# Attention scores of 64 rows per head, rebuilt as split products on all 128 rows

## The chip, the cores and the metric

The kernel runs on one core of a Trainium2 chip. A core has a matrix engine (TensorE, PE in the profile, with its weight loads listed apart as PEld), a vector engine (DVE), a scalar engine (ACT), GpSimd (POOL) and a queue that issues transfers (SP). Each engine works through its own instructions in order and waits on semaphores for the others. The metric is device time in microseconds (us), the median of the runs shown; lower is better.

## The reference

Two transformer blocks are computed for 256 tokens of width 2048, in float32. Only the two places where attention scores are formed matter here.

```python
# first block: 32 heads of 64, 4 key heads, window of 128, a sink per head
scores = jnp.einsum('bnqhgd,bnkhd->bnhgqk', q, kb) * (HEAD_DIM ** -0.5)
...
# second block, latent attention: 16 heads, a plain part of 128 and a rope part of 64
sc = (jnp.einsum('bqhd,bkhd->bhqk', qn, k_nope).astype(jnp.float32)
      + jnp.einsum('bqhr,bkr->bhqk', qr, k_rope).astype(jnp.float32)) * scale
```

In the first block the sum under a score runs over 64 numbers. In the second it runs over 128 and then over 64 more, whose key part (`k_rope`) is the same for all heads. A second attention in the second block (heads of 128) is not touched.

## The kernel before

**Layout.** Activations are kept transposed: a tile has 128 features on its rows (partitions) and the 256 tokens along it. A unit is a tile of 128 x 512, which holds two such halves, or the high part of one half beside its low part; there is a pool of 67 units (`NU`). In the first block one half of `q_a` holds two heads below each other, the first on rows 0 to 63 and the second on rows 64 to 127. In the second block one half of `q_r` holds the rope parts of two heads in the same way.

**Products.** The large products do not run in plain float32. Each operand is split into a high part, rounded to a shorter float type (F32R), and a low part, the rest; the product is the sum of high x high, high x low and low x high. A float32 product, where one is still used, is carried out by the compiler as two rows of the trace, a split one as one row. Weights come from memory in chunks (`w_raw`), ACT casts the high part (`w_hi`, L84) and DVE subtracts it to get the low part (`w_lo`, L85); each has four buffers of eight 128 x 128 tiles. `mm` (L195) issues every matmul, so most PE rows carry that one line; the names tell them apart. In a row such as `ps_g<-h,w_hi` the result lies in one of four PSUM banks of the kind g; scores go to two banks of the kind s, and transposes and the products with v to two banks of the kind t.

**Order of the work.** The gemms form one long stream on PE. Attention is put between their matmuls by `Interleave`: an attention is a Python generator, and after every so many weight tiles (`between.every`) one of the waiting generators is taken a step further. A scheduler under the kernel then places each engine's instructions in an order of its own, except for the few that are pinned; this order is fixed when the kernel is built.

**The steps that are touched.** `first_norm` (L455) scales keys into `k_a`, which holds four key heads, and values into `v_a`. `attend_a` (L470) is called 16 times, each for two heads: four score matmuls on 64 rows, two per head (queries 0 to 127 against keys 0 to 127, queries 128 to 255 against all 256), then `exps` (L396: DVE adds the bias and finds the smallest value, ACT takes the exponential), transposes and products with v. The two heads of a call stand on different rows and are issued in turn, the one behind the other. `attend_m` (L688) is called 8 times for two heads: first the plain part on 128 rows (`k_n`, `q_n`), then the rope part on 64 rows (`kr`, which lies in the tile `rb2_kr`, and `q_r`), added in the same bank. `norms` (L665) rotates `kr`, `rope_q` (L720) rotates `q_r`. `split_scaled` (L228) is the helper that writes a high part with ACT and a low part with DVE.

Of the kernel before, what the change touches and what calls it, by code (L numbers as in the profile page):

```python
# [9 lines left out]
F32 = mybir.dt.float32  # L10
# [157 lines left out]
def block_kernel(ctx, tc, order, w, xt, cols, bc, fg, cst, out):  # L168
# [227 lines left out]
    def exps(ps, table, scale, negmax, sums, init):  # L396
# [9 lines left out]
        return t  # L406

    def transposed(p, on_act=False):

        ps = bank("t")  # L410
        for j in range(3):
            nc.tensor.transpose(out=ps[:, j * P:j * P + P], in_=p[:, j * P:j * P + P], identity=ident)  # L412
        pt = unit("prob_t")[:, 0:384]
        if on_act:
            nc.scalar.copy(out=pt, in_=ps[:, 0:384])
        else:
            nc.vector.tensor_copy(out=pt, in_=ps[:, 0:384])
        return pt
# [32 lines left out]
    negsink = const.tile([P, 32], F32, name="negsink")  # L451
    k_a = unit("k_a")
    v_a = unit("v_a")

    def first_norm():  # L455
        for i in range(8):
            sq.add(x_t[i])
            if i % 2:
                yield
        nc.vector.tensor_copy(out=r_a, in_=rstd(sq.sums(), D))  # L460
        yield 2
        rows(r_a, rb)
        yield
        for j in range(2):
            scaled(half(k_a, j), ps_k[j], rb)
        for tb in range(2):
            nc.scalar.activation(out=half(v_a, tb), in_=half(ps_v, tb), func=AF.Copy, scale=r_a[:, tb:tb + 1])
        pin(nc.vector.tensor_scalar(out=negsink, in0=sinks, scalar1=-1.0, scalar2=None, op0=ALU.mult))

    def attend_a(j, q, o):  # L470
# [5 lines left out]
        pp = [bank("s") for _ in range(2)]  # L476
        for a, b, n in ((0, P, P), (P, S, S)):
            for e, ps in enumerate(pp):
                rng = slice(64 * e, 64 * e + 64)
                mm(ps[:, a:a + n], q[rng, a:b], k_a[rng, kt * S:kt * S + n], a == 0, a > 0)  # L480
        for e, ps in enumerate(pp):
# [32 lines left out]
    for j in range(16):  # L514
# [7 lines left out]
        for i, b in ((0, ps_0), (1, ps)) if j == 1 else ((j, ps),):  # L522
            if i % 2 == 0:
                q, o = unit("q_a"), unit("o_a")
                o_a.append(o)
            scaled(half(q, i), b, rb)
            between.add(attend_a(i, half(q, i), half(o, i)))

# [85 lines left out]
    rb2_kr = unit("rb2_kr")  # L614
    rb_2, kr = rb2_kr[:, 0:S], rb2_kr[:, S:]
    rb_lat = unit("rb_lat")
    rb_kv, rb_q = rb_lat[:, 0:S], rb_lat[:, S:]
# [47 lines left out]
    def norms(ps):  # L665
# [11 lines left out]
        yield  # L677
        rotate(kr)
    between.add(norms(ps))
    between.apart = 1  # L680
# [6 lines left out]

    def attend_m(j, qn, qr, kn, v):  # L688

        while j // 2 not in roped:  # L690
            yield
        negmax, sums, rec = sm("negmax"), sm("sums"), sm("rec")
        pp = [bank("s") for _ in range(2)]
        for e, ps in enumerate(pp):
            mm(ps[:, 0:P], qn[e][:, 0:P], kn[e][:, 0:P], True, False)
            mm(ps[:, P:384], qn[e][:, P:S], kn[e], False, False)
        for a, b, n in ((0, P, P), (P, S, S)):
            for e, ps in enumerate(pp):
                rng = slice(64 * e, 64 * e + 64)
                mm(ps[:, a:a + n], qr[rng, a:b], kr[rng, 0:n], False, a > 0)  # L700
        p = [exps(ps, tab_m, scale_m, negmax[:, 2 * e:2 * e + 2], sums[:, 2 * e:2 * e + 2], BIG)
# [18 lines left out]
    def rope_q(u, qr):  # L720
        yield
        for i in range(2):
            rotate(half(qr, i))
        roped.add(u)

    roped = set()

    for u in range(4):
# [20 lines left out]
        for i in range(4):  # L749
# [4 lines left out]
            if i % 2:  # L754
                between.add(attend_m(2 * u + i // 2, [half(qn[-1], e) for e in range(2)], half(qr, i // 2),
                                     [half(kn[i // 2], e) for e in range(2)],
# [314 lines left out]
```

## Time and profile before

| what | value |
|---|---|
| median of the runs shown | 2041.04 us (3 runs, 2039.53 to 2041.19) |
| the profiled execution's own time | 2042.15 us |
| its span, first to last instruction | 2040.4 us |
| granted TensorE clock, mean | 0.996 |
| PE busy | 2014.4 us, 99% of the span |
| DVE busy | 1304.3 us, 64% |
| ACT busy | 1071.6 us, 53% |
| transfers from memory | 360.98 MB, 178 GB/s over the span |

A group of rows in the profile names the line, the engine, the operation, result and operands, the shape of each and their count, and behind the bar the busy time, the mean time of one in ns, and the idle time of the engine ahead of them. In a timeline each row is a run of equal instructions: when the first starts, how long until the last ends, and how many there are. Matmul rows overlap, since the next starts before the last has ended; what one costs is therefore read from start to start, not from its own duration.

### The profile page before, as it was taken

What the parts mean: (1) busy time and instruction counts of PE and PEld (TensorE: products, weight loads), DVE (VectorE), ACT (ScalarE), POOL (GpSimd) and SP (SyncE); (2) the same over time, 40 slices, a digit from 0 to 9 for tenths busy, and PEclk for the clock granted to TensorE, in tenths of its full rate; (3) what the DMA queues carried; (4) which work ended last, traced back from release to release, by engine and by line L of the source; (5) the groups of instructions that cost most, each with busy time, mean ns of one, the idle gap of its engine ahead of it and who ended that gap; (6) DMA issues with size and microseconds to landing.
All of it is one profiled execution on the core that took longest, in us unless ns stands there. A gap on an engine that the chain in (4) does not pass through costs nothing.

```text
span 2040.4 us, 28289 instructions
## 1 busy us (share of the span) xinstructions
PE 2014.4 (99%) x11290; PEld 1744.5 (85%) x11290; DVE 1304.3 (64%) x2129; ACT 1071.6 (53%) x1818; POOL 19.2 (1%) x25
## 2 busy tenths in 40 slices
PE   7999999999999999999999999999999999999998
PEld 6787888888888888888888888888888888888886
DVE  6768865887766655566575767666666666555543
ACT  6767655656545444455465445464445554444443
POOL 0000000000000000000000000000000000000000
PEclk9999999999999999999999999999999999999999
DMA  7343456353444555545545555545555555555553
GB/s 295 119 152 128 166 186 232 109 186 125 149 159 171 186 186 187 193 171 174 183 166 186 187 193 193 185 173 187 189 193 194 187 186 187 191 220 186 196 196 103
DMA packets 53667, 364.89 MB, mean 179 GB/s; under 512 B 6240, under 2 KB 7136, under 8 KB 10400
## 3 DMA queue, kind: packets, MB, share of 16 engines
q1 hardware_dynamic: 52560, 361.07, 49.5%
q8 instruction: 88, 1.44, 0.3%
q0 software_dynamic: 400, 1.31, 0.2%
q10 hardware_dynamic: 576, 0.72, 0.1%
q14 instruction: 43, 0.35, 0.1%
HBM read 360.98 MB, written 2.10 MB: 178 GB/s over the span
## 4 chain that ended last, share of the span: by engine, by line
PE 96%; DVE 1%; ACT 1%; issue 1%; DMA 0%; SPq 0%; POOL 0%; POOLq 0%; ACTq 0%; DVEq 0%
PE ps_g L195 89%; PE ps_s L195 5%; PE ps_t L195 2%; PE ps_t L412 1%; DMA w_raw<-w 0%; ACT prob L404 0%; DVE w_lo L85 0%; ACT w_hi L84 0%; PE ps_t L810 0%; PE ps_t L906 0%; POOL rstd L277 0%; PE ps_t L786 0%; DVE prob L400 0%; DVE prob L496 0%; SPq L217 0%
## 5 line engine op out<-in xcount | busy, mean ns | idle before, releaser
L85 DVE TENSOR_TENSOR w_lo<-w_raw,w_hi 128x1024 fp32r<-128x1024 f32 (+1 forms) x676 | 825.6, 1222 | 320.0 <-ACT w_hi L84 289.9
L84 ACT CAST w_hi<-w_raw 128x1024 fp32r<-128x1024 f32 (+1 forms) x676 | 708.3, 1048 | 352.7 <-PE ps_g L195 269.6
L195 PE MATMUL ps_g<-h,w_hi 128*128 128x512 f32 x3064 | 750.1, 393 | 8.1 <-ACT w_hi L84 6.7
L195 PEld LDWEIGHTS ps_g<-h,w_hi 128*128 128x128 f32 x3064 | 561.9, 189 | 120.2 <-ACT w_hi L84 6.7
L195 PEld LDWEIGHTS ps_g<-h,w_lo 128*128 128x128 f32 x3064 | 395.2, 191 | 20.3 <-issue 4.0
L195 PE MATMUL ps_g<-h,w_lo 128*128 128x256 f32 x3064 | 408.4, 284 | 0.9 <-DVE k_a L198 0.9
L195 PE MATMUL ps_g<-w_hi,act 128*128 128x512 f32 x704 | 216.8, 389 | 0.0
L195 PEld LDWEIGHTS ps_g<-w_hi,act 128*128 128x128 f32 x704 | 132.1, 188 | 27.5
L381 ACT COPY ffn<-ps_g 128x256 f32<-128x256 f32 x86 | 31.8, 373 | 200.9 <-PE ps_g L195 200.9
L195 PE MATMUL ps_g<-w_lo,act 128*128 128x512 f32 x352 | 136.9, 389 | 0.0
L198 DVE TENSOR_TENSOR ffn<-ffn,ps_g 128x256 f32<-128x256 f32 x86 | 36.0, 421 | 144.4 <-ACT ffn L381 144.4
L195 PE MATMUL ps_g<-w_hi,h 128*128 128x512 f32 x256 | 79.4, 389 | 0.0
L195 PEld LDWEIGHTS ps_g<-w_lo,act 128*128 128x128 f32 x352 | 66.1, 188 | 13.7
L404 ACT ACTIVATE prob<-prob,negmax 128x128 f32<-128x128 f32 (+1 forms) x128 | 56.7, 445 | 24.1 <-DVE negmax L400 23.5
L195 PE MATMUL ps_g<-y_m,w_hi 128*128 128x512 f32 x256 | 63.8, 391 | 0.0
L195 PE MATMUL ps_g<-y_d,w_hi 128*128 128x512 f32 x256 | 61.2, 391 | 0.0
L195 PE MATMUL ps_g<-g,w_hi 128*128 128x512 f32 (+1 forms) x240 | 57.8, 377 | 0.0
L195 PEld LDWEIGHTS ps_g<-w_hi,h 128*128 128x128 f32 x256 | 48.1, 188 | 9.9
L195 PE MATMUL ps_g<-mg,w_hi 128*128 128x512 f32 x224 | 56.0, 391 | 0.0
L195 PEld LDWEIGHTS ps_g<-y_d,w_hi 128*128 128x128 f32 x256 | 47.0, 188 | 9.1
L195 PEld LDWEIGHTS ps_g<-y_m,w_hi 128*128 128x128 f32 x256 | 47.0, 188 | 9.1
L195 PE MATMUL ps_g<-c,w_hi 128*128 128x512 f32 x208 | 53.6, 400 | 0.0
(238 smaller groups left out, 1859.2 us busy)
## 6 DMA issues: line engine op xcount, KB each, us to landing
w_raw<-w SPq DMA_DIRECT2D x337, 1024.0 KB, 4.8
w_raw<-w SPq DMA_DIRECT2D x5, 512.0 KB, 7.8
out<-x2n SPq DMA_DIRECT2D x8, 256.0 KB, 3.1
x_t<-xt SPq DMA_DIRECT2D x7, 256.0 KB, 7.8
fgt<-fg POOLq DMA_DIRECT2D x4, 256.0 KB, 5.5
w_raw<-w SPq DMA_DIRECT2D x2, 256.0 KB, 4.6
x_t<-xt SPq DMA_DIRECT2D x2, 128.0 KB, 3.2
lam<-bc POOLq DMA_DIRECT2D x1, 256.0 KB, 6.1
```

The lines of the kernel that those rows point to most:

```text
L84: a = nc.scalar.copy(out=hi[:, q], in_=src[:, q])
L85: b = nc.vector.tensor_tensor(out=lo[:, q], in0=src[:, q], in1=hi.bitcast(F32)[:, q], op=ALU.subtract)
L195: nc.tensor.matmul(out=o, lhsT=a, rhs=b, start=start, stop=stop, skip_group_check=True)
L198: nc.vector.tensor_tensor(out=o, in0=a, in1=b, op=op)
L381: nc.scalar.copy(out=o, in_=ps[:, S:])
L404: nc.scalar.activation(out=t[:, a:b], in_=t[:, a:b], func=AF.Exp, scale=-1.0, bias=negmax[:, qb:qb + 1], accum_out=sums[:, qb:qb + 1])
L412: nc.tensor.transpose(out=ps[:, j * P:j * P + P], in_=p[:, j * P:j * P + P], identity=ident)
```

## The change

For each half of a query tile, the new helper `stacked` writes a unit `q_s` with one half per head. The head's 64 rows are cast to the high part in place (ACT), and the low part is written by DVE on the other 64 rows. So high and low parts of one head stand below each other on 128 rows. Keys get the matching form once: each key head has a unit (`k_s0` to `k_s3`) whose first half is the high part on both sets of 64 rows, and whose second half is the low part on both sets. For the rope part `kr`, which already stands twice below itself, a plain `split_scaled` gives `kr_s`. `stacked_scores` multiplies the stacked queries with the high keys and then with the low keys. This covers all four products of high and low parts.

Per call of an attention, 4 float32 matmuls on 64 rows become 8 split ones on 128 rows: 4 with 128 columns of keys and 4 with 256. In the trace that is 8 rows against 8.

```diff
--- before.py
+++ after.py
@@ -405,6 +405,23 @@
                                  accum_out=sums[:, qb:qb + 1])
         return t
 
+    def stacked(src):
+
+        t = unit("q_s", F32R)
+        for e in range(2):
+            own, other = slice(64 * e, 64 * e + 64), slice(64 - 64 * e, 128 - 64 * e)
+            hi = t[own, e * S:e * S + S]
+            nc.scalar.copy(out=hi, in_=src[own])
+            nc.vector.tensor_tensor(out=t[other, e * S:e * S + S], in0=src[own], in1=hi.bitcast(F32),
+                                    op=ALU.subtract)
+        return [t[:, 0:S], t[:, S:]]
+
+    def stacked_scores(ps, q, k, first):
+
+        for a, b, n in ((0, P, P), (P, S, S)):
+            for o in (0, S):
+                mm(ps[:, a:a + n], q[:, a:b], k[:, o:o + n], first and a + o == 0, a + o > S)
+
     def transposed(p, on_act=False):
 
         ps = bank("t")
@@ -449,7 +466,7 @@
     r_a = const.tile([P, 2], F32, name="r_a")
     rb = unit("rb_a")[:, 0:S]
     negsink = const.tile([P, 32], F32, name="negsink")
-    k_a = unit("k_a")
+    kk = []
     v_a = unit("v_a")
 
     def first_norm():
@@ -461,8 +478,15 @@
         yield 2
         rows(r_a, rb)
         yield
+        k_a = unit("k_a")
         for j in range(2):
             scaled(half(k_a, j), ps_k[j], rb)
+            for e in range(2):
+                own, other = slice(64 * e, 64 * e + 64), slice(64 - 64 * e, 128 - 64 * e)
+                t = unit(f"k_s{2 * j + e}", F32R)
+                split_scaled(half(k_a, j)[own], None, t[own])
+                nc.scalar.copy(out=t[other], in_=t[own].bitcast(F32))
+                kk.append(t)
         for tb in range(2):
             nc.scalar.activation(out=half(v_a, tb), in_=half(ps_v, tb), func=AF.Copy, scale=r_a[:, tb:tb + 1])
         pin(nc.vector.tensor_scalar(out=negsink, in0=sinks, scalar1=-1.0, scalar2=None, op0=ALU.mult))
@@ -474,10 +498,8 @@
         negmax, sums, t = sm("negmax"), sm("sums"), sm("tiny")
         p = []
         pp = [bank("s") for _ in range(2)]
-        for a, b, n in ((0, P, P), (P, S, S)):
-            for e, ps in enumerate(pp):
-                rng = slice(64 * e, 64 * e + 64)
-                mm(ps[:, a:a + n], q[rng, a:b], k_a[rng, kt * S:kt * S + n], a == 0, a > 0)
+        for e, ps in enumerate(pp):
+            stacked_scores(ps, q[e], kk[2 * kt + e], True)
         for e, ps in enumerate(pp):
             slope = 2.0 ** (-8.0 * (heads[e] + 1) / 32)
             bias = unit("bias")[:, 0:384]
@@ -524,7 +546,7 @@
                 q, o = unit("q_a"), unit("o_a")
                 o_a.append(o)
             scaled(half(q, i), b, rb)
-            between.add(attend_a(i, half(q, i), half(o, i)))
+            between.add(attend_a(i, stacked(half(q, i)), half(o, i)))
 
     lam = unit("lam")
     nc.gpsimd.dma_start(out=lam, in_=bc[:, 32:544])
@@ -613,6 +635,7 @@
     r2sq = const.tile([P, 2], F32, name="r2sq")
     rb2_kr = unit("rb2_kr")
     rb_2, kr = rb2_kr[:, 0:S], rb2_kr[:, S:]
+    kr_s = unit("kr_s", F32R)
     rb_lat = unit("rb_lat")
     rb_kv, rb_q = rb_lat[:, 0:S], rb_lat[:, S:]
 
@@ -676,6 +699,7 @@
         yield
         yield
         rotate(kr)
+        split_scaled(kr, None, kr_s)
     between.add(norms(ps))
     between.apart = 1
     cq, r_q, fin_q = latent(((m, gemm("in_2", m, h)) for m in range(6)), 6, G_Q, rb_q)
@@ -685,19 +709,18 @@
     y_m = [None] * 16
     scale_m = 1.0 / math.sqrt(192.0)
 
-    def attend_m(j, qn, qr, kn, v):
+    def attend_m(j, qn, kn, v):
 
         while j // 2 not in roped:
             yield
+        qr = qr_s.pop(j)
         negmax, sums, rec = sm("negmax"), sm("sums"), sm("rec")
         pp = [bank("s") for _ in range(2)]
         for e, ps in enumerate(pp):
             mm(ps[:, 0:P], qn[e][:, 0:P], kn[e][:, 0:P], True, False)
             mm(ps[:, P:384], qn[e][:, P:S], kn[e], False, False)
-        for a, b, n in ((0, P, P), (P, S, S)):
-            for e, ps in enumerate(pp):
-                rng = slice(64 * e, 64 * e + 64)
-                mm(ps[:, a:a + n], qr[rng, a:b], kr[rng, 0:n], False, a > 0)
+        for e, ps in enumerate(pp):
+            stacked_scores(ps, qr[e], kr_s, False)
         p = [exps(ps, tab_m, scale_m, negmax[:, 2 * e:2 * e + 2], sums[:, 2 * e:2 * e + 2], BIG)
              for e, ps in enumerate(pp)]
         nc.vector.reciprocal(out=rec, in_=sums)
@@ -721,9 +744,11 @@
         yield
         for i in range(2):
             rotate(half(qr, i))
+            qr_s[2 * u + i] = stacked(half(qr, i))
         roped.add(u)
 
     roped = set()
+    qr_s = {}
 
     for u in range(4):
         kn = []
@@ -752,7 +777,7 @@
                 qn.append(unit("q_n"))
             scaled(half(qn[-1], i), ps, rb_q)
             if i % 2:
-                between.add(attend_m(2 * u + i // 2, [half(qn[-1], e) for e in range(2)], half(qr, i // 2),
+                between.add(attend_m(2 * u + i // 2, [half(qn[-1], e) for e in range(2)],
                                      [half(kn[i // 2], e) for e in range(2)],
                                      [[t[:, e * P:e * P + P] for t in v] for e in (i - 1, i)]))
 
```

The three places below show the order in which the rows stand on an engine. `h_187` and the like are the split input tiles of the first block, `c_0_4091` and the like those of the second, `ps_*` are banks, and a number behind x is how many rows stand in sequence.

PE, the first attention of the first block, before:

```order
L195 MATMUL ps_g<-h_187,w_hi 128x512
L195 MATMUL ps_s<-k_a,q_a 128x128 x2
L195 MATMUL ps_s<-k_a,q_a 128x256 x2
L195 MATMUL ps_g<-h_200,w_hi 128x512
L195 MATMUL ps_g<-h_217,w_hi 128x512
L195 MATMUL ps_g<-h_230,w_hi 128x512
```

PE, the first attention of the first block, after:

```order
L195 MATMUL ps_g<-h_200,w_hi 128x512
L195 MATMUL ps_g<-h_217,w_hi 128x512
L195 MATMUL ps_s<-k_s_493,q_s 128x128 x2
L195 MATMUL ps_s<-k_s_493,q_s 128x256 x2
L195 MATMUL ps_s<-k_s_497,q_s 128x128 x2
L195 MATMUL ps_s<-k_s_497,q_s 128x256 x2
L195 MATMUL ps_g<-h_230,w_hi 128x512
L195 MATMUL ps_g<-h_247,w_hi 128x512
```

The scores of this call stand 34 gemm rows later than before (18 with 512 columns, 16 with 256), and the two heads no longer take turns.

ACT, from the scaling of the keys on, before:

```order
L381 COPY k_a<-ps_g 128x256 x2
L467 ACTIVATE v_a<-ps_s,r_a 128x256 x2
L381 COPY q_a<-ps_g 128x256 x2
L484 ACTIVATE bias<-tab_a 128x384 x2
L404 ACTIVATE prob,sums<-prob,negmax 128x128
```

ACT, from the scaling of the keys on, after:

```order
L381 COPY k_a<-ps_g 128x256 x2
L232 CAST k_s_493<-k_a 64x256
L232 CAST k_s_497<-k_a 64x256
L232 CAST k_s_504<-k_a 64x256
L488 CAST k_s_493<-k_s_493 64x512
L488 CAST k_s_497<-k_s_497 64x512
L488 CAST k_s_504<-k_s_504 64x512
L232 CAST k_s_508<-k_a 64x256
L491 ACTIVATE v_a<-ps_s,r_a 128x256 x2
L488 CAST k_s_508<-k_s_508 64x512
L381 COPY q_a<-ps_g 128x256 x2
L84 CAST w_hi<-w_raw 128x1024 x2
```

The eight casts of the keys stand ahead of the copies of the first two query halves, and two weight casts now stand right behind these.

PE, an attention of the second block (the fourth of eight), before:

```order
L195 MATMUL ps_s<-k_n,q_n 128x128
L195 MATMUL ps_s<-k_n,q_n 128x256
L195 MATMUL ps_s<-rb_kr,q_r 128x128 x2
L195 MATMUL ps_s<-rb_kr,q_r 128x256 x2
L195 MATMUL ps_g<-c_0_4091,w_hi 128x512
```

PE, the same attention after:

```order
L195 MATMUL ps_s<-k_n,q_n 128x128
L195 MATMUL ps_s<-k_n,q_n 128x256
L195 MATMUL ps_s<-kr_s,q_s 128x128 x2
L195 MATMUL ps_s<-kr_s,q_s 128x256 x2
L195 MATMUL ps_s<-kr_s,q_s 128x128 x2
L195 MATMUL ps_s<-kr_s,q_s 128x256 x2
L195 MATMUL ps_g<-c_0_4252,w_hi 128x512
```

Here the rope scores stay at the same place in the stream, and only their form changes.

## The prediction

> **What bounds the kernel now.** I read the page's busy times first, then the chain that ended last, then PE's waits, then PE's timeline at the places of the change.
>
> ```profile
> span 2040.4 us, 28289 instructions
> PE 2014.4 (99%) x11290; PEld 1744.5 (85%) x11290; DVE 1304.3 (64%) x2129; ACT 1071.6 (53%) x1818; POOL 19.2 (1%) x25
> PE 96%; DVE 1%; ACT 1%; issue 1%; DMA 0%; SPq 0%; POOL 0%; POOLq 0%; ACTq 0%; DVEq 0%
> ```
>
> PE is busy nearly always and carries 96% of the chain. A microsecond taken from PE's stream is a microsecond of the whole, as long as what feeds PE keeps up. The next rows (stretches with busy time of PE, PEld, DVE, ACT, POOL; then two rows of waits) cover the two stages that the change touches.
>
> ```profile
> 50.00:230.00 180.00, 179.10 (x1103) 143.70 (x1102) 131.62 (x368) 124.84 (x326) 0.70 (x1) 0.99 0.38 136
> 450.00:570.00 120.00, 120.00 (x698) 101.78 (x696) 92.62 (x219) 70.61 (x160) 0.00 (x0) 1.00 0.39 139
> 60.00:70.00 10.00, 9.42 (x59) 7.48 (x58) 9.93 (x34) 9.24 (x28) 0.00 (x0) 1.00 0.35 117
> ACT w_hi L84 <- PE ps_g L195: 269.6, 197, 3.0
> PE ps_s L195 <- DVE q_a L198: 0.3, 1, 0.3
> ```
>
> PE idles 0.9 us in the first stage and not at all in the second. ACT waits 269.6 us in all for PE to free a weight buffer, so the weight casts run ahead of need. DVE and ACT have room on average, but between 60 and 70 us they are full.
>
> **What a score group costs now.** The marginal cost is read from start to start. First the price of ordinary gemm rows:
>
> ```profile
> 447.74 1.75 PE L195 MATMUL ps_g<-c,w_hi 128*128 128x512 f32 x7
> 449.33 1.59 PE L195 MATMUL ps_g<-c,w_lo 128*128 128x256 f32 x12
> 450.76 2.46 PE L195 MATMUL ps_g<-c,w_hi 128*128 128x512 f32 x10
> ```
>
> Seven rows of 512 columns take 449.33 - 447.74 = 1.59 us, 0.227 each; twelve of 256 take 1.43, 0.119 each. Now the scores of two calls of `attend_a`, and two single heads further on:
>
> ```profile
> 53.50 0.93 PE L195 MATMUL ps_s<-k_a,q_a 64*128 64x128 f32 x8
> 54.35 2.55 PE L195 MATMUL ps_g<-h,w_hi 128*128 128x512 f32 x10
> 56.83 0.93 PE L195 MATMUL ps_s<-k_a,q_a 64*128 64x128 f32 x8
> 57.69 2.18 PE L195 MATMUL ps_g<-h,w_lo 128*128 128x256 f32 x16
> ...
> 191.26 0.92 PE L195 MATMUL ps_s<-k_a,q_a 64*128 64x128 f32 x4
> 192.10 1.22 PE L195 MATMUL ps_g<-h,w_lo 128*128 128x256 f32 x8
> 193.25 0.92 PE L195 MATMUL ps_s<-k_a,q_a 64*128 64x128 f32 x4
> ```
>
> From 53.50 to 56.83 is 3.33 us; ten gemm rows of it are worth 2.27, so a pair of heads costs 1.06. Of that the eight score rows take 0.85 (to 54.35) and 0.21 is change-over: the ten rows behind take 2.48 instead of 2.27. A single head costs 193.25 - 191.26 - 8 x 0.119 = 1.04. So two heads in turn cost what one costs: they run at the same time on the two halves of the array. The rope part behaves alike:
>
> ```profile
> 457.68 1.48 PE L195 MATMUL ps_s<-k_n,q_n 128*128 128x128 f32 x8
> 459.08 0.93 PE L195 MATMUL ps_s<-rb_kr,q_r 64*128 64x128 f32 x8
> 459.94 1.20 PE L195 MATMUL ps_g<-c,w_hi 128*128 128x512 f32 x4
> 460.97 0.39 PE L195 MATMUL ps_g<-w_hi,c 128*128 128x512 f32 x1
> ```
>
> It takes 0.86, the four gemm rows behind it 1.03 instead of 0.91, and the change-over ahead of it hides in the 1.40 of the plain part. The row shapes are those of `attend_a`, so I take 1.06 again.
>
> The count is 14 pairs and 4 single heads in the first block (the order on PE leaves two calls split) and 8 pairs in the second: 22 x 1.06 + 4 x 1.04 = 27.5 us. This is removed.
>
> **What the new scores cost.** Each pair gets 4 split rows of 256 columns and 4 of 128, all on 128 rows. Split rows of 256 stand outside the gemms too:
>
> ```profile
> 649.42 0.28 PE L195 MATMUL ps_t<-v_hi,a_hi 128*128 128x256 f32 x1
> ...
> 650.49 1.72 PE L195 MATMUL ps_g<-y_m,w_lo 128*128 128x256 f32 x13
> ```
>
> Nine such rows (three products for each of three blocks) fill 649.42 to 650.49, 0.119 each, with no change-over on either side. So 256 columns cost 0.12. No split row of 128 columns is in this trace. Its bound from above is that 0.12, since it streams half as much. From below, the matmuls with a single column show what a row costs that streams nothing (one window, cut after two, three and four rows):
>
> ```profile
> 417.84 0.28 PE L195 MATMUL ps_t<-ones,sq 128*128 128x1 f32 x2
> 417.84 0.39 PE L195 MATMUL ps_t<-ones,sq 128*128 128x1 f32 x3
> 417.84 0.50 PE L195 MATMUL ps_t<-ones,sq 128*128 128x1 f32 x4
> ```
>
> Each further row adds 0.11 with one column, which must be its weight load. So a row of 128 columns lies between 0.11 and 0.12; I take 0.115. A pair is then 4 x 0.12 + 4 x 0.115 = 0.94, and 24 pairs are 22.6 us (22.1 to 23.0). The gain on PE is 27.5 - 22.6 = 4.9 us (4.5 to 5.4).
>
> [...]
>
> **What is added elsewhere.** Per query half ACT casts twice and DVE subtracts twice, 64x256 each: 48 on each engine over 24 calls. Keys add 8 casts and 4 subtractions, `kr` one of each. No 64-row form is in the trace; the same operations on 128 rows are:
>
> ```profile
> L232 ACT CAST act<-ffn 128x256 fp32r<-128x256 f32 x44 | 17.9, 407 | 1.8 <-DVE ffn L198 1.8
> L233 DVE TENSOR_TENSOR act<-ffn,act 128x256 fp32r<-128x256 f32 x44 | 18.5, 420 | 0.9 <-ACT act L232 0.9
> L84 ACT CAST w_hi<-w_raw 128x512 fp32r<-128x512 f32 x4 | 2.4, 617 | 4.4 <-DMA w_raw<-w 4.4
> ```
>
> Whether 64 rows are cheaper than 128 is not shown; I take the price whole, and half of it is the low end. In the first block DVE gets 36 x 0.42 = 15.1 us, 131.6 to 147 of 180; ACT gets 36 x 0.41 + 4 x 0.62 = 17.2, 124.8 to 142. In the second DVE goes from 92.6 to 100 of 120. No transfer is added, and the rows on SP and POOL are unchanged. On average the cover holds, and I cost this work at nothing except where the new wait bites.
>
> That is the start. Scores now wait for `q_s`; behind them on PE stand all gemm rows. On ACT the eight key casts stand ahead of the copies of the first query halves.
>
> ```profile
> 47.27 0.84 ACT L467 ACTIVATE v_a<-ps_s,r_a 128x256 f32<-128x256 f32 x2 [1.79 <-DVE r_a L460]
> 48.00 0.65 ACT L381 COPY q_a<-ps_g 128x256 f32<-128x256 f32 x2
> 50.22 0.17 DVE L468 TENSOR_SCALAR negsink<-sinks 128x32 f32<-128x32 f32 x1
> 57.25 1.03 ACT L84 CAST w_hi<-w_raw 128x1024 fp32r<-128x1024 f32 x1
> ```
>
> Keys are ready at 50.22 (the row behind them on DVE). From there ACT needs 4 x 0.41 + 4 x 0.62 for keys, 0.84 for `v_a`, 0.65 for query copies, 2 x 1.03 for weights and 2 x 0.41 for the first `q_s`: 58.7, and one subtraction more is 59.1. PE had its first scores at 53.50 and now has 18 x 0.227 + 16 x 0.119 = 6.0 us of gemm ahead of them: 59.5. So the first scores come about in time. Weights are no later: the cast that began at 57.25 may begin at 54.8. Calls two and three follow within a few microseconds on full engines, and I take 0.5 us of new waits for all of it (0 to 3).
>
> **The sum.** -4.9 + 0.5 = -4.4 us. Against the profiled execution's own 2042.15 (1.7 above its span) that is 2037.7; this execution stands 1.1 above the median, and against the median 2041.04 I get 2036.6.
>
> **Rivals.**
> - The change-over stays. If the 0.21 comes from putting any foreign group with a wait into the stream, and not from the 64-row form, a new pair costs 0.94 + 0.21 = 1.15, 24 make 27.6, and with the waits it ends at 2041.6: no change. The nine rows at 649.42 speak against it.
> - Slower, rows of 128 columns run at the price of float32. A split row could fall back to several passes when it is short; the nearest row is the 512-column gemm, 0.227. Then 24 x (4 x 0.12 + 4 x 0.227) = 33.3, 5.8 more than before, and with 0.5 of waits 2047.3. It decides against the change once a short row costs over 0.16. The single-column rows show only that a load does not force it.
> - Slower, the split of queries and keys reaches PE where DVE is full (60 to 70 us, 9.93 of 10): keys and the first three calls bring 10 x 0.42 = 4.2 us to DVE, and the same may befall the first calls of the second block, 5 x 0.42 = 2.1. In full that is 6.3 against 4.9: 2042.4. It decides from 4.9 us of new waits on. The start worked out above speaks against it.
> - Faster, short rows cost their stream alone, 0.06: 24 x 0.72 = 17.3, with waits 2031.3. This needs weight loads hidden better than the single-column rows show. [...]
>
> **Chances.** About 0.2%, 4.1 us, is what can be told from no change here. My sum holds, with 0 to 3 us of waits, at 0.66, of which 0.47 is faster and 0.19 within 0.2%. Change-over stays: 0.08, the same. Price of float32: 0.08, slower. Split reaches PE: 0.09, 0.04 the same and 0.05 slower. Short rows cheaper: 0.09, faster. Rounded, that is 0.56, 0.31 and 0.13. The range goes from just above the cheapest short rows, 2032.0, to the full price of the splits, 2042.5; it leaves out the float32 price and part of the cheapest case.
>
> **What would show it.** Right: score rows on 128 rows with starts 0.12 apart, gemm rows at their usual distance on both sides, the 16 calls within 50 to 230 us about 3.5 us shorter in sum, PE's waits for `q_s` under 1 us. Wrong: short rows over 0.16 apart, rows of PE that wait for `q_s` or for late weight casts between 55 and 80 us, or a change-over of 0.2 us that stays.

## The result and the profile after

The changed kernel takes 2048.61 us, the median of 4 runs (2048.04 to 2050.74), against 2040.8 us for the kernel before in the same session. The ratio is 1.004, with a 95% interval of 1.0028 to 1.0053. It is slower by about 8 us, where 2036.6 us was forecast, and it lies above the range. The profiled execution took 2048.33 us.

The page of the changed kernel, busy times and the chain that ended last:

```profile
span 2046.4 us, 28399 instructions
PE 2014.0 (98%) x11290; PEld 1755.0 (86%) x11290; DVE 1325.7 (65%) x2182; ACT 1094.7 (53%) x1875; POOL 18.4 (1%) x25
PE 93%; DVE 3%; ACT 2%; issue 1%; DMA 0%; SPq 0%; POOL 0%; ACTq 0%; POOLq 0%; DVEq 0%
```

PE is busy for as long as before (2014.0 against 2014.4 us), where 4.9 us less was forecast, the span is 6 us longer, and DVE and ACT carry 5% of the chain instead of 2%. So PE's idle time grew, and something else took up the gain in its busy time. The stretches of the prediction, with one more (20 us from 430 us on), show where; the columns are busy time of PE, PEld, DVE, ACT and POOL, then the granted clock:

```profile
50.00:230.00 180.00, 176.10 (x1091) 148.11 (x1091) 145.09 (x402) 141.93 (x369) 0.75 (x1) 0.99 0.38 132
60.00:70.00 10.00, 10.00 (x62) 8.64 (x61) 9.87 (x36) 9.74 (x33) 0.00 (x0) 1.00 0.61 211
430.00:450.00 20.00, 16.62 (x78) 13.90 (x78) 12.50 (x29) 8.37 (x14) 0.69 (x1) 0.91 0.37 125
450.00:570.00 120.00, 119.09 (x695) 104.69 (x694) 99.22 (x229) 74.61 (x167) 0.00 (x0) 1.00 0.41 148
```

PE now idles 3.9 us in the first block (0.9 before), 3.4 us between 430 and 450 us, and 0.9 us in the second block. Its waits from 50 to 230 us (the first three rows) and from 430 to 570 us (the rest):

```profile
PE ps_s L195 <- DVE negmax L400: 2.2, 3, 1.2
PE ps_t L429 <- ACT prob_t L432: 1.0, 1, 1.0
PE ps_t L429 <- DVE prob_t L434: 0.3, 1, 0.3
PE ps_g L195 <- DVE k_n L198: 3.4, 1, 3.4
PE ps_s L195 <- DVE negmax L400: 0.6, 1, 0.6
PE ps_s L195 <- DVE q_s L415: 0.2, 1, 0.2
```

Only one of them is for the new tile `q_s`, 0.2 us. The others are for operations that the kernel before had too, and that now come late.

To see how much time each stage lost, the same four rows of PE can be looked up in both kernels: the first matmul of the squares behind the first block, the same in the norms of the second block, the first `k_n` scores, and the first `qk_d` scores. First the kernel before (its `k_n` row, at 457.68, stands in the prediction):

```profile
354.75 0.39 PE L195 MATMUL ps_t<-ones,sq 128*128 128x1 f32 x3
433.23 0.50 PE L195 MATMUL ps_t<-ones,sq 128*128 128x1 f32 x4
433.60 0.47 PE L195 MATMUL ps_g<-w_hi,c 128*128 128x512 f32 x1
629.43 0.38 PE L195 MATMUL ps_s<-qk_d 128*128 128x128 f32 x2
```

And after:

```profile
355.64 0.39 PE L195 MATMUL ps_t<-ones,sq 128*128 128x1 f32 x3
433.31 0.50 PE L195 MATMUL ps_t<-ones,sq 128*128 128x1 f32 x4
437.18 0.47 PE L195 MATMUL ps_g<-w_hi,c 128*128 128x512 f32 x1 [3.38 <-DVE k_n L198]
439.57 1.05 PE L195 MATMUL ps_g<-w_hi,c 128*128 128x512 f32 x2
440.43 0.63 PE L195 MATMUL ps_g<-w_lo,c 128*128 128x512 f32 x1
462.89 1.48 PE L195 MATMUL ps_s<-k_n,q_n 128*128 128x128 f32 x8
635.30 0.38 PE L195 MATMUL ps_s<-qk_d 128*128 128x128 f32 x2
```

| stretch | before | after | difference |
|---|---|---|---|
| start to the squares behind the first block | 354.75 | 355.64 | +0.9 |
| to the squares of the second block | 78.48 | 77.67 | -0.8 |
| to the first `k_n` scores | 24.45 | 29.58 | +5.1 |
| to the first `qk_d` scores | 171.75 | 172.41 | +0.7 |

With what lies behind, that is the 6.0 us by which the two spans differ. The medians of the runs lie 7.8 us apart, so one execution of each tells this only to within some 2 us. One part of that is the second line of the table: no touched code runs in it, but each trace has a stretch at a lower clock there (mean grant 0.93 before and 0.96 after), and it isn't equally long in every execution. The first line holds such a part too. PE reaches the row that waits for `k_a`, ahead of all that the change adds, at 49.45 before and at 48.84 after; over all runs of this document it comes between 48.40 and 51.11. From that row on, the first block is 306.80 us long after and 305.30 before, 1.5 us longer.

**The score rows themselves.** Their price came out as forecast. The first call of the first block, and a later one with the gemm rows behind it:

```profile
58.86 1.08 PE L195 MATMUL ps_s<-k_s,q_s 128*128 128x128 f32 x8
...
156.07 1.08 PE L195 MATMUL ps_s<-k_s,q_s 128*128 128x128 f32 x8
156.99 2.08 PE L195 MATMUL ps_g<-h,w_lo 128*128 128x256 f32 x16
158.90 1.09 PE L195 MATMUL ps_s<-k_s,q_s 128*128 128x128 f32 x8
```

The eight score rows take 156.99 - 156.07 = 0.92. The sixteen gemm rows behind them take 1.91, 0.119 each, as anywhere else, so nothing is left of the change-over there. Over the undisturbed pairs, with what they leave on the rows beside them, it is about 0.95 in the first block and 0.92 in the rope part, where 0.94 was forecast. (Most rope rows follow directly on the plain part and then take 1.11 to the next row, while the plain part takes 1.12 instead of 1.40; both together, with the rows behind, take 2.23 to 2.24 instead of 2.36 to 2.38.) The first scores also start without a wait, at 58.86; the prediction had worked out 59.5 for them.

So the cheaper rows are there. With the counts of the prediction they are worth 14 x 1.06 + 4 x 1.04 - 16 x 0.95 = 3.8 us in the first block and 8 x (1.06 - 0.92) = 1.1 us in the second. Since the first block is 1.5 us longer all the same, it holds about 5.3 us of new losses; the second block's attention holds 1.1 + 0.7 = 1.8; and the place at 433 us holds 5.1. These 12.2 us stand against a forecast of 0.5; by the medians of the runs it is 7.8 + 4.9 = 12.7. PE's idle time shows only part of it: 3.0 us more in the first block, 3.4 at 433 us and 0.9 in the second block. Another 1.8 us is the clock at 433 us, as shown next. The rest, some 3 us, is rows that stand further apart; where the two heads of a call are set apart, a head costs 0.56 to 0.57 instead of 0.46 at three of four such calls. It isn't traced row by row.

**The place at 433 us.** Here `norms` of the second block rotates `kr`, and the change splits it right behind. DVE and ACT after the change:

```profile
433.56 1.04 ACT L84 CAST w_hi<-w_raw 128x1024 fp32r<-128x1024 f32 x1 [2.69 <-PE ps_g L195]
434.51 0.40 ACT L232 CAST kr_s<-rb_kr 128x256 fp32r<-128x256 f32 x1
434.82 1.19 ACT L381 COPY k_n<-ps_g 128x256 f32<-128x256 f32 x4
...
435.15 1.22 DVE L85 TENSOR_TENSOR w_lo<-w_raw,w_hi 128x1024 fp32r<-128x1024 f32 x1
436.29 0.42 DVE L233 TENSOR_TENSOR kr_s<-rb_kr,kr_s 128x256 fp32r<-128x256 f32 x1
436.62 0.74 DVE L198 TENSOR_TENSOR k_n<-k_n,ps_g 128x256 f32<-128x256 f32 x2
```

Before, the same copies and the first addition:

```profile
430.71 0.64 ACT L381 COPY k_n<-ps_g 128x256 f32<-128x256 f32 x2
432.98 0.41 DVE L198 TENSOR_TENSOR k_n<-k_n,ps_g 128x256 f32<-128x256 f32 x1
```

PE's next gemm needs the bank that the additions of `k_n` read. Before, ACT made its first two copies at 430.71. After, the scheduler has put a weight cast and the cast of `kr_s` ahead of all four. That weight cast waits 2.69 us until PE frees a buffer, so the copies wait with it; on DVE a weight subtraction and the one of `kr_s` stand ahead of the additions as well. PE then waits 3.38 us. Behind the wait its rows run at half clock: 440.43 - 439.57 is 0.86 for two rows that take 0.45 elsewhere. A mean grant of 0.91 over 20 us is 1.8 us lost, and 3.4 + 1.8 is the 5.1 of the table, within rounding. The same wait with the rope part alone, below, has a low clock behind it too (0.83); without the wait the grant is 1.00 over these 20 us, before the change and with `kr` split later. Why it falls is not shown.

**Places in the first block.** One of them, with PE, then ACT after the change:

```profile
103.46 0.55 PE L429 MATMUL ps_t<-ident,prob 128*128 128x128 f32 x3 [1.02 <-ACT prob_t L432]
...
101.05 1.03 ACT L84 CAST w_hi<-w_raw 128x1024 fp32r<-128x1024 f32 x1
...
102.09 0.81 ACT L414 CAST q_s<-q_a 64x256 fp32r<-64x256 f32 x2
102.93 0.48 ACT L432 COPY prob_t<-ps_t 128x384 f32<-128x384 f32 x1
```

PE's next transposes need the bank that the copy `prob_t` empties. Two casts of a later call's queries, 0.81 us, stand directly ahead of it on ACT, behind a weight cast, and PE waits 1.02 us. The waits for `negmax` are of the same kind on DVE. That is what the trace suggests; whether the casts and subtractions are the cause is what the runs below test. The rows of this one place were not changed by themselves.

### The profile page after: what moved, and what is told of

The parts are those of the page before. It is cut to its first block, busy times and chain, and to the rows that moved or that the text cites. A ratio compares the mean times of both kernels' runs of the same rounds, so it can differ in the third digit from the quotient of the medians.

```text
span 2046.4 us, 28399 instructions
## 1 busy us (share of the span) xinstructions
PE 2014.0 (98%) x11290; PEld 1755.0 (86%) x11290; DVE 1325.7 (65%) x2182; ACT 1094.7 (53%) x1875; POOL 18.4 (1%) x25
## 4 chain that ended last, share of the span: by engine, by line
PE 93%; DVE 3%; ACT 2%; issue 1%; DMA 0%; SPq 0%; POOL 0%; ACTq 0%; POOLq 0%; DVEq 0%
PE ps_g L195 86%; PE ps_s L195 4%; PE ps_t L195 2%; DVE w_lo L85 1%; PE ps_t L429 1%; ACT w_hi L84 1%; ACT prob L404 0%; DVE prob L400 0%; DMA w_raw<-w 0%; ACT bias L506 0%; DVE q_s L415 0%; ACT q_s L414 0%; DVE k_n L198 0%; POOL rstd L277 0%; PE ps_t L835 0%
```

## The experiments

The theory (**waits**): the new score rows are as cheap as forecast, and the loss is old work that comes late behind the new casts and subtractions, at 433 us above all. The rival (**dear rows**): something about the new rows themselves costs time. All ratios are against the kernel before on the same chip. The first four runs share one set of runs of it (2041.47 us), the next four another (2041.4).

### The rope part alone

```diff
-        for e, ps in enumerate(pp):
-            stacked_scores(ps, q[e], kk[2 * kt + e], True)
+        for a, b, n in ((0, P, P), (P, S, S)):
+            for e, ps in enumerate(pp):
+                rng = slice(64 * e, 64 * e + 64)
+                mm(ps[:, a:a + n], q[rng, a:b], k_a[rng, kt * S:kt * S + n], a == 0, a > 0)
```

`attend_a` and the scaling of the keys are as before; the second block is changed.

> Only the rope part of the second block is changed; the first block is as before. Theory of the waits (the new rows cost what was forecast, the loss is new waits): 8 pairs save 8 x 0.12 = 1.0 us, the wait of PE at 433 us for k_n costs 3.4 and the half clock behind it 1.7, the other new waits of the second block 1.8: +5.9 us, about 2046.7. Rival, dear rows (the new score rows themselves cost more, 5.8 us over 24 pairs): 8 of 24 pairs, +1.9 us, about 2042.7.

Measured: 2047.44 us, ratio 1.0029 (1.0018 to 1.004). The wait of PE for `k_n` is there, 3.4 us long as in the whole change, and the clock stays low for longer. The stretch from 430 us on:

```profile
430.00:450.00 20.00, 16.62 (x75) 13.91 (x74) 11.77 (x27) 7.96 (x14) 0.69 (x1) 0.83 0.34 116
```

This is what the theory of waits expected. Eight calls of cheaper rows do not make up for one wait and what it does to the clock.

### The first block alone

The reverse: `attend_m`, `rope_q` and `norms` as before.

```diff
-        split_scaled(kr, None, kr_s)
...
-        for e, ps in enumerate(pp):
-            stacked_scores(ps, qr[e], kr_s, False)
+        for a, b, n in ((0, P, P), (P, S, S)):
+            for e, ps in enumerate(pp):
+                rng = slice(64 * e, 64 * e + 64)
+                mm(ps[:, a:a + n], qr[rng, a:b], kr[rng, 0:n], False, a > 0)
```

> Only the first block is changed; the rope part is as before. Theory of the waits: the scores save 3.9 us, new waits between 60 and 200 us give back 5.6: +1.7 us, about 2042.5, and no wait of PE at 433 us. Dear rows: 16 of 24 pairs, +3.9 us, about 2044.7.

Measured: 2042.95 us, ratio 1.0007 (0.9999 to 1.0016). PE has no wait between 430 and 570 us. The two halves together (0.29% and 0.07%) give the 0.4% of the whole within the intervals. The first block alone gains nothing.

### `kr` split later

The split of `kr` moves from `norms` to the first `rope_q`, behind the products of the keys.

```diff
         rotate(kr)
-        split_scaled(kr, None, kr_s)
...
         for i in range(2):
             rotate(half(qr, i))
+        if u == 0:
+            split_scaled(kr, None, kr_s)
```

> The whole change, but kr is split in the first rope_q, some 25 us later, in place of in norms. Theory of the waits: the additions to k_n are no longer behind the chain of the rope key on DVE, so the wait of 3.4 us at 433 us and the stretch at half clock behind it are gone: 5.1 us less than the changed kernel, about 2043.5. Rival, general load (ACT and DVE are late there because of all the splits, wherever kr is split): the wait stays and the time too, about 2048.6.

Measured: 2043.52 us, ratio 1.0011 (1.0002 to 1.0019). The place at 433 us, on PE:

```profile
434.54 0.50 PE L195 MATMUL ps_t<-ones,sq 128*128 128x1 f32 x4
434.90 0.47 PE L195 MATMUL ps_g<-w_hi,c 128*128 128x512 f32 x1
```

The gemm follows the squares as closely as before the change, and the clock between 430 and 450 us is 1.00. Moving two instructions of 0.4 us gave back some 6 us by the ratios (1.004 to 1.0011), 5.1 by the medians. That settles this part of the loss. What remains is still slower than before.

### The queries not split

```diff
+    kept = []
     def stacked(src):
-        t = unit("q_s", F32R)
+        if kept:
+            return kept
+        t = const.tile([P, 512], F32R, name="q_s")
...
-        return [t[:, 0:S], t[:, S:]]
+        kept.extend([t[:, 0:S], t[:, S:]])
+        return kept
```

On top of the last one, all 24 calls use the stacked queries of the first, so that 46 casts and 46 subtractions fall away and the score rows stay.

> As the version with the later split of kr, but the queries are stacked once, for the first half of a query tile, and all later scores use that one tile: the splitting of the other 23 query halves on ACT and DVE is left out, the matmul rows on PE are all there. Theory of the waits: PE's gain stands alone, 4.9 us below the kernel before less at most 1 us of waits, 2036 to 2037. Dear rows: 5.8 us above the kernel before, about 2046.6.

Measured: 2038.84 us, ratio 0.9989 (0.998 to 0.9998), 4.5 us under the last one by the ratios. PE's waits in the first block:

```profile
PE ps_t L434 <- DVE prob_t L439: 1.4, 2, 0.8
...
PE ps_s L195 <- DVE negmax L400: 0.6, 1, 0.6
```

Without the query splits, which the prediction had costed at nothing beside 0.5 us, the kernel is 4.5 us faster. (No score waits for its own queries here either, so the figure holds that too.) The expectation of 2036 to 2037 was missed by 2 us: some waits stay without the splits, at places that the new order on the engines made.

### Three ways to relieve the engines

All on top of the later `kr`. First, the low parts of the queries on POOL instead of DVE:

```diff
-            nc.vector.tensor_tensor(out=t[other, e * S:e * S + S], in0=src[own], in1=hi.bitcast(F32),
+            nc.gpsimd.tensor_tensor(out=t[other, e * S:e * S + S], in0=src[own], in1=hi.bitcast(F32),
```

> The whole change with the later split of kr, and the 48 subtractions that make the low parts of the queries run on POOL in place of DVE. What is left after the later split is 7.4 us of new waits in the first block and behind 460 us. Theory DVE is late: DVE loses 20 us of work, half or more of these waits go, 2039 to 2041. Theory ACT is late (casts of the queries stand ahead of copies that PE waits for): no change, about 2043.5. Theory POOL is too slow for it: the scores wait for the low part, over 2045.

Measured: 2050.48 us, ratio 1.0039 (1.0027 to 1.0052). The last theory of the three holds: POOL is too slow for it. Its subtractions (durations in ns, lowest, median and highest) take 0.74 and 0.79 us in the median, where DVE takes 0.42. In the second block alone PE waits 2.6 us for them:

```profile
L415 POOL TENSOR_TENSOR q_s<-q_a,q_s x32: 722/737/1631, 57.8 to 165.5; 64x256 fp32r<-64x256 f32 x32
L415 POOL TENSOR_TENSOR q_s<-q_r,q_s x16: 724/792/2481, 461.8 to 564.1; 64x256 fp32r<-64x256 f32 x16
```

Second, more distance between the steps of an attention in the first block:

```diff
-            between.every, between.apart = 8, 3
+            between.every, between.apart = 8, 4
```

> The whole change with the later split of kr, and the steps of an attention of the first block four ticks apart in place of three, so that its transposes and products with v stand some 2.8 us of gemm later. Theory of late results (PE reaches transposes and scores before ACT and DVE are done, as they have more to do): most of the 5.6 us of waits of the first block goes, about 2038.5 to 2040. Rival, full throughput (ACT and DVE cannot do the work of the stretch in time, wherever the steps stand): no change, 2043 to 2044.

Measured: 2043.04 us, ratio 1.0006 (0.9997 to 1.0015), within the rival's range. The wait for `prob_t` shrinks from 1.0 to 0.2 us, but the scores now wait 3.0 us for `negmax` in three places, where 2.2 stood. Steps of three attentions still stand next to each other, only further from the next group.

Third, the 32 scalings of the bias on POOL instead of ACT:

```diff
-            nc.scalar.activation(out=bias, in_=tab_a, func=AF.Copy, scale=8.0 * slope)
+            nc.gpsimd.tensor_scalar(out=bias, in0=tab_a, scalar1=8.0 * slope, scalar2=None, op0=ALU.mult)
```

> The whole change with the later split of kr, and the 32 scalings of the bias table of the first block run on POOL in place of ACT, which takes 32 x 0.47 = 15 us from ACT, about what the casts of the queries there add (13). Theory ACT is late: the waits of the first block fall by half or more, 2039 to 2041. Theory DVE is late: no change, about 2043.5.

Measured: 2044.55 us, ratio 1.0014 (1.0005 to 1.0023). ACT's work from 50 to 230 us falls from 141.2 to 128.8 us, almost to what it was before the change, and nothing is gained, though no instruction waits for the scalings on POOL. So the load of ACT alone isn't what makes results late.

### The load without the rows

The kernel before, with the stacked query tiles of the first block written and never read.

```diff
+            stacked(half(q, i))
             between.add(attend_a(i, half(q, i), half(o, i)))
```

> The kernel before, which also makes the stacked tile of every query half of the first block but does not read it: ACT gets 32 casts and DVE 32 subtractions, the scores are the old ones. Theory of load (the added work delays other results that PE waits for): 3 to 6 us above the kernel before, 2044 to 2047. Rival, the chain (the waits come from scores that now stand behind cast and subtraction): 0 to 1 us above, 2041 to 2042.5.

Measured: 2044.78 us, ratio 1.0014 (1.0005 to 1.0023). No matmul depends on these 32 casts and 32 subtractions, and still they cost 2.9 us by the ratios. The stretch from 50 to 230 us:

```profile
50.00:230.00 180.00, 177.22 (x1080) 141.32 (x1080) 142.05 (x391) 134.94 (x350) 0.70 (x1) 0.99 0.38 136
```

PE idles 2.8 us in it. But in this execution the wait for `k_a`, 0.94 us, falls inside the stretch, while it ends ahead of 50 us in the kernel before. Without it the idle time is 1.8 us, against 0.9 before. The other 2 us are rows: four calls have their two heads set apart, where two had. These are the two more:

```profile
130.14 0.92 PE L195 MATMUL ps_s<-k_a,q_a 64*128 64x128 f32 x4
131.64 0.92 PE L195 MATMUL ps_s<-k_a,q_a 64*128 64x128 f32 x4 [0.15 <-DVE negmax L400]
...
168.03 0.92 PE L195 MATMUL ps_s<-k_a,q_a 64*128 64x128 f32 x4 [0.21 <-DVE negmax L400]
...
169.24 0.92 PE L195 MATMUL ps_s<-k_a,q_a 64*128 64x128 f32 x4
```

At the prices of the prediction that is 2 x (2 x 1.04 - 1.06) = 2.0 us. So casts and subtractions that nobody reads do delay PE, with no wait for a new operand. But what they cost here is mostly the pairing of heads, 1.02 a call, and the split rows of the changed kernel gain little from pairing (0.10 to 0.11 a head at three of its four calls with heads apart): little more than the 0.9 us of waits can be carried over to it. Why the scheduler sets these heads apart isn't shown.

### The attentions spread out

The attentions start in groups of three. On top of the later `kr`, a new attention may begin only three ticks behind the last one, and steps are four ticks apart, so that scores, transposes and products with v of three attentions stand evenly in the stream. The same on the kernel before is the control.

```diff
-            if not self.queue:
+            if not self.queue or self.ticks < self.begun + self.gap:
                 return
+            self.begun = self.ticks
...
-            between.every, between.apart = 8, 3
+            between.every, between.apart, between.gap = 8, 4, 3
```

The changed kernel:

> The full change with the split of kr moved behind the key products (2043.5 us), and the attentions of the first block begun no sooner than three ticks of the stream apart, their steps four ticks apart. Scores, transposes and products with v of three attentions then stand evenly, one each in three ticks, where they stood in groups of three. Theory of bursts: the 5 us of waits that the change brought to the first block (PE idle 3.9 us between 50 and 230 us, 0.9 before) come from three attentions that split, subtract and take exponentials in neighbouring ticks, where DVE and ACT are full; spread out they have room (145 and 142 us of work in 180), most of the waits go, and the time is 2038.5 to 2040. Theory of throughput: DVE and ACT have too much to do in the whole stage and the waits only change their place; 2043 to 2044.

The kernel before:

> The kernel before with the same spreading alone, as the control. It has only 0.9 us of waits of PE between 50 and 230 us, so by the theory of bursts there is little to gain: 2040 to 2041.5, or about 2039 if the two calls whose heads the scheduler had set apart now run at the same time (2 x 1.04 us). If spreading saved as much here as on the changed kernel, it would save something else than the waits of the splits.

Measured, both against the same runs of the kernel before (2041.4 us): the changed kernel spread out takes 2039.77 us, ratio 0.9993 (0.9984 to 1.0002); the kernel before spread out takes 2037.2 us, ratio 0.998 (0.997 to 0.9989). First the changed one:

```profile
50.00:230.00 180.00, 177.34 (x1114) 151.94 (x1114) 149.75 (x408) 143.69 (x372) 0.70 (x1) 1.00 0.40 138
```

Then the control:

```profile
50.00:230.00 180.00, 180.00 (x1120) 146.98 (x1119) 135.88 (x376) 127.39 (x329) 0.70 (x1) 0.99 0.39 139
```

The spread takes 3.7 us from the changed kernel, as the theory of bursts expected. But it takes 4.1 us from the kernel before, which was not expected in this size, and the expectation for the control says what that means: it saves something else than the waits of the splits. In the kernel before, PE now waits 0.0 us between 50 and 230 us, and all 16 calls have their two heads together, at 1.06 each; 14 x 1.06 + 4 x 1.04 - 16 x 1.06 = 2.0 us come from that and 0.9 from the waits. The other 1.2 us are not accounted for. In the changed kernel PE's idle time in this stretch falls only from 3.8 us (with the later `kr`) to 2.7, and the rows of all 16 calls stand together there too. So the idle time that the change adds is 2.9 us in groups and 2.7 us spread out: by these traces bursts do not explain it. About 2 of the 3.8 us that the split rows seemed to gain in the first block can be had without them, by keeping the heads of a call together. With both kernels spread, the change still costs 2.6 us; in groups, with the later `kr`, it cost 2.2. The best kernel here is the one before, spread out.

### What the load costs once it is spread

Two runs to divide these 2.6 us: the unused tiles again, on the spread kernel before (32 casts and 32 subtractions; the 64 of each at the start of the text on record is a slip), and the change in the first block alone, spread.

The first kernel, against the kernel before:

```diff
-            between.every, between.apart = 8, 3
+            between.every, between.apart, between.gap = 8, 4, 3
...
+            stacked(half(q, i))
             between.add(attend_a(i, half(q, i), half(o, i)))
```

> The kernel before with the attentions of the first block spread, and beside it the unused stacked tiles of the queries (64 casts and 64 subtractions short of nothing else: 32 of each): the load of the splits without the new score rows. Without the spread this load cost 3.4 us (2044.78 against 2041.4). Theory of bursts: the load costs because it falls where DVE and ACT are full, so spread out it costs at most 1 us more than the spread kernel before, 2037 to 2038.5. Theory of throughput: the load costs its 3 us again, 2040 to 2041.

The second, against the change:

```diff
-            between.every, between.apart = 8, 3
+            between.every, between.apart, between.gap = 8, 4, 3
...
-        split_scaled(kr, None, kr_s)
...
-            stacked_scores(ps, qr[e], kr_s, False)
+                mm(ps[:, a:a + n], qr[rng, a:b], kr[rng, 0:n], False, a > 0)
```

> The change in the first block alone, spread; the rope part as before. Theory that the second block gives about 0.8 us of what is left (DVE late with the smallest values at two calls): 0.5 to 1 us below the whole change spread out (2039.77), so 2038.8 to 2039.3, still above the spread kernel before (2037.2) because of 2.0 us of waits for copies of the transposed weights. Theory that all of the rest lies in the first block: 2039.8.

Measured (before 2040.94 us): the unused tiles 2038.6 us, ratio 0.9988 (0.9979 to 0.9997); the first block alone 2038.91 us, ratio 0.9989 (0.998 to 0.9998). Against the spread kernel before (0.998, beside other runs of the kernel before) the load costs 0.08%, 1.6 us, where it cost 2.9 us in groups. That lies between the two theories, and intervals of 0.09% to each side leave room for both. The traces tell more. All 16 calls have their heads together in this run, and PE idles 0.8 us from 50 to 230 us, where it idled 0.0 without the tiles; in groups the tiles added 0.9. By these traces the waits are nearly the same, and what the spread spares this load is the lost pairing.

The first block alone is 0.8 us under the whole change by the ratios, as expected, but that is inside the intervals. The traces agree with it: from the first `k_n` scores to the first `qk_d` scores it is 172.54 us with the whole change spread out, and 171.75 with the first block alone, as in the kernel before. So the second block's part is a loss of about that size also once `kr` is out of the way. The first block keeps two waits for `prob_t`, 2.0 us together. The longer one, in the whole change spread out, DVE's copy and then PE:

```profile
168.16 0.55 DVE L437 COPY prob_t<-ps_t 128x384 f32<-128x384 f32 x1
168.77 0.87 PE L198 MATMUL ps_t<-prob_t,v_a 128*64 128x256 f32 x8 [1.39 <-DVE prob_t L437]
```

PE wants the transposed weights, and DVE copies them only after a weight subtraction and the minima of another call. If these 2.0 us went, the change in the first block would, by estimate, stand level with the spread kernel before. An order that does this was not tried, and stays open.

## Why the prediction was wrong

**The price of the rows: right.** 22.6 us were forecast for 24 pairs; 16 x 0.95 + 8 x 0.92 is 22.6. The change-over of 0.21 went with the 64-row form, so the rival in which it stays is out, and so is the one of float32 prices: a row of these pairs costs 0.115 to 0.12 in the mean. Without the change-over the new form would have lost: the eight old rows of a pair alone take 0.85, and a new pair costs 0.95 in the first block and 0.92 in the second.

**The start: right.** First scores at 58.86 without a wait, PE busy for all 10 us from 60 to 70 us. The place that the prediction feared is the one where nothing happened. (The 54.8 that it gave for the next weight cast doesn't follow from its list, which comes to 55.8; the cast came at 55.03, ahead of 57.25 either way.)

**The step that failed: "I take 0.5 us of new waits for all of it (0 to 3)".** The new losses were about 12 us: 7.3 of idle time of PE, 1.8 of lower clock, and some 3 in rows that stand further apart. Two things stand behind it.

First, the prediction followed the new operand, `q_s`, and asked when PE would wait for that. PE waited 0.2 us for it in all. What it missed is that each cast or subtraction stands ahead of something else in the order of its engine (at 433 us the first copies of `k_n` waited out the 2.69 us of the weight cast ahead of them), and that the scheduler chose new places for the old work too. Averages ("DVE 131.6 to 147 of 180") hid this: the unused tiles alone, which brought DVE to 142 of 180, cost 2.9 us, 0.9 of it in waits. That the splits cost time is shown by leaving them out (4.5 us); which instruction delays which in the first block is read from the trace and not tested. In the first block this is the third rival, "the split reaches PE where DVE is full". It named the mechanism, but its place was wrong (all but 0.3 us of the waits lie past 90 us) and it counted only keys and first calls. That its sum, 2042.4 us, is near the 2043.5 that is left once `kr` is moved is luck. It was given 0.09.

Second, the two instructions of `kr` were counted ("`kr` one of each") and costed at nothing, without a row of that place. At 433 us the gemms run with the weight casts close ahead, ACT's next cast waits for PE to free a buffer, and PE waits for a copy behind that cast. The 0.4 us of the split did not cost 0.4 us; the new order made ACT wait for PE while PE needed ACT, and the clock fell on top (a grant of 0.91 over 20 us): 5.1 us by the trace, about 6 by the ratios. No rival had this.

**A smaller one.** The 27.5 us removed held four single heads at 1.04. The prediction saw that two heads in turn cost what one costs, yet booked the gain of 2 us to the new form of the rows. The control shows that it belongs to keeping heads together.

**The direction.** The lower price of the rows was real and the cover for 48 casts and 48 subtractions was not. A warning stood in the rows quoted: between 60 and 70 us PE lost 0.6 us in the kernel before, with DVE at 9.93 of 10, though its load was 73% on average (131.6 of 180 us).

## What to carry to other kernels

When a change adds work to engines that PE waits for, look not only at who needs the new result, but at every old instruction that now stands behind it on the same engine, above all next to a cast that itself waits for PE (2.69 us here, and PE then waited 3.38); read the built order at each place that the change touches, however small its part there. Average room on DVE and ACT was no cover here: with DVE busy for 142 of 180 us the unused tiles cost 2.9 us, 0.9 of it in waits. When a new order makes the changed kernel faster, try it on the kernel before too: here the spread saved 4.1 us without the change and 3.7 with it, so it was a gain of the order and no cure for the splits.

## What was not expected of the hardware

- Score rows are not evenly spaced. The first call of the first block again, in windows that end at 58.93 and at 59.05:

```profile
58.86 0.33 PE L195 MATMUL ps_s<-k_s,q_s 128*128 128x128 f32 x2
58.86 0.50 PE L195 MATMUL ps_s<-k_s,q_s 128*128 128x128 f32 x3
```

  Two short rows have started within 0.07 us, and the third row comes at 59.03. By the starts in the trace the distances go 0.06, 0.11, 0.17, 0.12 and so on in turn. A short row was followed in 0.06 here, half of the 0.119 of a row of 256 columns. The mean of the four is 0.115, which the prediction had taken for a short row and nearly for a long one. That the rows behind pay for the weight loads is a reading of this pattern and not tested.
- A cast or subtraction of 64 rows cost here what one of 128 rows costs:

```profile
L414 ACT CAST q_s<-q_a 64x256 fp32r<-64x256 f32 x32 | 12.8, 402 | 11.8 <-DVE q_a L198 11.4
L415 DVE TENSOR_TENSOR q_s<-q_a,q_s 64x256 fp32r<-64x256 f32 x32 | 13.4, 420 | 3.7 <-ACT q_s L414 2.8
```

  402 and 420 ns, against 407 and 420 on 128 rows in the prediction. So splitting a tile head by head took two instructions of the full price.
- The same wait of 3.38 us was followed by a stretch at half clock of very different length: a grant of 0.91 over 20 us in the changed kernel (0.09 x 20 x 2 = 3.6 us at half) and of 0.83 with the rope part alone (6.8 us). These are one execution each.
